# A two-layer decoder on one Trainium2 core: the last output projection by seven block products in place of eight, and the last scan begun sooner

## The chip, the core and the metric

The kernel runs on one core of a Trainium2 chip. Five engines of the core work side by side, each through its own queue of instructions in order: PE (TensorE, matrix products), DVE (VectorE), ACT (ScalarE), POOL (GpSimd) and SP (SyncE, which here only issues DMAs). They meet at semaphores. Data comes from HBM by DMA into SBUF (128 partitions); matrix products land in PSUM. The metric is the device time of one execution in microseconds (us); the lower the better.

## The reference: what is computed

There are 512 tokens of width 2048 and two residual layers: differential attention, then RWKV-7 time mixing. The change lies at the end of the second.

```python
def rwkv7_mixer(h, ...):
    p = h @ w_in                                  # 2048 -> 4*2048 + 192
    p = p + (token_shift(p) - p) * mu
    r, k, v, g, dw, da = jnp.split(p, RW_SPLITS, axis=-1)
    ...
    y = wkv7_scan(rh, heads(decay), kh, vh, -kk, kk * ah)     # 32 heads of 64, over 512 tokens
    ...                                           # normalised per head, weighted, bonus term added
    y = y.reshape(B, T, RW_WIDTH).astype(h.dtype) * jax.nn.silu(g)
    return y @ w_out, v_first                     # 512 x 2048 times 2048 x 2048

x = x + out                                       # the residual
```

## The kernel before

**Products of split numbers.** Every large product takes float32 data in three passes. Each operand is cast to a shorter float format (`hi`, ACT), and the rest is taken off by a subtraction (`lo = x - hi`, DVE). `mm3` (line 106) then issues hi·hi, hi·lo and lo·hi into one PSUM tile. `split_w` (line 87) does the cast (L96) and the subtraction (L97) for a piece of weights that `load_w` (line 73) has brought by a DMA from the SP queue. The raw weights have three buffers (`wraw`), `wh` and `wl` two each. `split_row` (line 403) does the same for a row of activations, into tiles `hH` and `hL` with sixteen buffers each.

**The order of the work.** The program is written in the framework's tile language. Each instruction gets a priority by its place in the program, raised by a fixed number inside `high_priority`; a scheduler fixes the order of every engine's queue when the program is built, by priority among those instructions whose inputs it holds ready and whose buffers it holds free. `issue_after(m)` puts instructions of the same engine behind matmul m.

**The second layer** walks over 16 pairs of heads (128 channels each). For each pair the projections `proj(0..3, j)` (48 matmuls each) give r, k, v and the gate; a small triangular solve runs on DVE (`t_solve`, line 830, tile `Tm`), its result goes through HBM (`td`) and comes back in 4 DMAs as `TT`; `t_combine` (line 860) finishes it with two groups of 32 small matmuls (tile `px`); `scan_pair` (line 950) then steps through 8 chunks of 64 tokens, with three small matmuls a chunk (L961, L972, L979, tile `sm`). In a chunk the state `VS` is updated on DVE (L983) from `sm` and from `Sg`, which POOL makes by one scaling (L970) after two copies into `SA` (L967). So that PE is not held up, these steps are strewn among the large products by a `Chain` (line 114): `tick` counts the matmuls of `mm3`, and every `yield n` in a chain's steps asks for n matmuls before the next step. A chain only counts once the chain before it is done. For the last pair (j = 15) the call is `chain(g, j, p, 80, 4, 4)`: 80 matmuls before the first step, 4 between the steps of a chunk.

**The last output projection.** `y` (channels x tokens) is 16 K tiles of 128 channels. Rows 0 to 13 lie in HBM (`yd2`); they are loaded and split once. Row 14 is made just before, row 15 only when the last scan is done. The weights are taken in four blocks of 512 columns; each block has four PSUM tiles (4 x 128 tokens; two of them are called `pp`, two `pt`) and runs over K in 8 pieces of 2 K tiles: one cast and one subtraction of 128 x 1024, then 24 matmuls of 128 x 512. At the end of a block four additions on DVE (L1126) add the residual, which comes by DMA from `xd`, and the results are stored from the ACT queue. In the first block the last scan runs between the matmuls; its row 15 joins as the last K tile.

Of the kernel before, what the change touches and what calls it, by code (L numbers as in the profile page):

```python
# [13 lines left out]
F32 = mybir.dt.float32  # L14
F32R = mybir.dt.float32r
# [3 lines left out]
ALU = mybir.AluOpType  # L19
# [4 lines left out]
P = 128  # L24
D = 2048
T = 512
KT = D // P
NT = T // P
# [10 lines left out]
AHEAD, SCAN, SOLVE = 2000, 3000, 4000  # L39
# [63 lines left out]
    return [(win, h * 256, 256), (win, D + h * 256, 256)]  # L103


def mm3(nc, out, aH, aL, bH, bL, start, stop, g=None):
    for a, b, s, e in ((aH, bH, start, False), (aH, bL, False, False), (aL, bH, False, stop)):
        m = nc.tensor.matmul(out, a, b, start=s, stop=e)  # L108
        if g:
            tick(g, m)  # L110
    return m
# [909 lines left out]
def group_norm(g, j, p):  # L1021
    p.chain.finish(g)
    nc, w, yc = g.nc, g.work, p.yc
    NG = 2 * NT
    sq = w.tile([P, NG, C], F32, name="ysq", tag="thg", bufs=1)
    nc.scalar.activation(sq[:], yc[:], AF.Square)
    var = g.small.tile([P, NG], F32, name="var", tag="var")
    nc.vector.reduce_sum(var[:], sq[:], AX.X)
    nc.vector.tensor_scalar(var[:], var[:], 1.0 / C, GN_EPS, ALU.mult, ALU.add)
    rs = g.small.tile([P, NG], F32, name="rsg", tag="rsg")  # L1030
    rsqrt(g, rs[:], var[:], NG, "r8")
    nc.vector.tensor_mul(yc[:], yc[:], rs[:, :, None].to_broadcast([P, NG, C]))
# [8 lines left out]
    nc.vector.scalar_tensor_tensor(p.y[:], ps[:], g.prm["hgw"][:, j : j + 1], p.y[:], ALU.mult, ALU.add)  # L1041


def layer1(g, aps):
    nc, tc = g.nc, g.tc
    with ExitStack() as cx:
# [23 lines left out]
        for j in range(D // P):  # L1070
# [30 lines left out]
                gated(g, j - LAG, pairs[j - LAG], gate(g, j - LAG, proj(3, j - LAG)))  # L1101
            if j + 1 < D // P:
                r = receptances(j + 1)
        chain(g, j, p, 80, 4, 4)
        gated(g, j - 2, pairs[j - 2], gate(g, j - 2, proj(3, j - 2)))
        gps = proj(3, j - 1)
        group_norm(g, j - 1, pairs[j - 1])
        finish_y(g, j - 1, pairs[j - 1])
        row = gated(g, j - 1, pairs[j - 1], gate(g, j - 1, gps), True)
        gt = gate(g, j, proj(3, j))  # L1110
        rows = split_rows(g, g.yd2, ("r", "k", "th0", "th1"), 1, j - 1) + [row]

        def all_rows(n, _):
            if n >= KT and len(rows) < KT:
                group_norm(g, j, p)
                finish_y(g, j, p)
                rows.append(gated(g, j, p, gt, True))

        yH, yL = Rows(rows, 0), Rows(rows, 1)
        for cb in range(4):  # L1120
            cs = slice(cb * 512, (cb + 1) * 512)
            pts = unit_tok(g, yH, yL, [(aps["rw_w_out"][0], cb * 512, 512)], 512, 2, more=all_rows)
            for t in range(NT):
                xr = w.tile([P, 512], F32, name="xr1", tag=("r", "k", "th0", "th1")[t], bufs=1)
                nc.sync.dma_start(out=xr[:], in_=g.xd[t * P : (t + 1) * P, cs])
                nc.vector.tensor_add(xr[:], xr[:], pts[t][:])  # L1126
                nc.scalar.dma_start(out=aps["out"][t * P : (t + 1) * P, cs], in_=xr[:])


@with_exitstack  # L1130
def body(ctx, tc, nc, aps):
    g = Ctx()
    g.nc, g.tc = nc, tc
    g.last, g.first = None, []
    g.chains, g.later, g.state = [], [], None
# [39 lines left out]
```

## Time and profile before

| | |
|---|---|
| Time, median of three runs (lowest to highest) | 2236.04 us (2233.57 to 2239.77) |
| The profiled execution's own time | 2235.41 us |
| Its span, first to last instruction | 2233.7 us |
| mean granted TensorE clock in it | 0.995 |
| DMA over the span | mean 100 GB/s |
| The four blocks of the last projection (us) | 55.06, 43.52, 43.52, 43.56 |
| DVE, ACT, POOL busy in the second block (us) | 12.53, 8.44, 0.00 |

The profile is of one execution. Busy time of an engine counts its instructions from start to end; matmuls are pipelined, so a matmul lasts longer than the distance to the next one, and the distance is the better measure of what it costs. A row of a timeline gives start and duration (us), engine, line, operation, written tile, read tiles and shape, in square brackets the idle time ahead of it and what ended that. A row that ends with x12 holds twelve instructions that follow each other. In a grouped view a row ends with the count, the busy time, the mean duration (ns) of one, and the idle time of that engine ahead of them. A row for a tile gives the minimum, the median and the maximum duration (ns).

### The profile page before, as it was taken

The numbers are of one execution on the slowest core, as the hardware profiler recorded it, in microseconds if no ns is written. First come the engines' busy times: TensorE is split into PE (matmuls) and PEld (weight loads), VectorE is DVE, ScalarE is ACT, GpSimd is POOL, SyncE is SP. The second block draws the span as 40 slices with busy tenths as digits, with TensorE's granted clock in tenths as the row PEclk, the third lists the DMA queues.
The fourth block names the chain that finished last, engine by engine and source line by source line (L and its number), as shares of the span: only waits on it lengthen the run. The fifth ranks groups of instructions, "written<-read, shape, count | busy, mean of one in ns | idle before, by whom it ended". The sixth has DMA issues, their size and how long they took to land. (4 is left out here: it accounts for less than half of the span.)

```text
span 2233.7 us, 33774 instructions
## 1 busy us (share of the span) xinstructions
PE 2184.1 (98%) x12260; PEld 1770.4 (79%) x12260; DVE 1374.9 (62%) x3666; ACT 1005.1 (45%) x2065; POOL 297.4 (13%) x672
## 2 busy tenths in 40 slices
PE   8999999999999999989999999999999999999999
PEld 6888888888888878877777777787777777777887
DVE  5555646455564664245667787777777877777322
ACT  5443434334343452225455555555455556545211
POOL 0000000000000000000323133333322233331000
PEclk9999999999999999999999999999999999999999
DMA  6222222222222254332423333333333333435333
GB/s 180 94 86 96 85 95 95 85 95 85 95 85 95 91 194 132 115 113 74 102 68 83 88 88 86 86 91 99 90 81 81 97 88 78 107 93 156 123 132 113
DMA packets 290730, 224.46 MB, mean 100 GB/s; under 512 B 47732, under 2 KB 255748, under 8 KB 290564
## 3 DMA queue, kind: packets, MB, share of 16 engines
q1 hardware_dynamic: 275892, 195.74, 30.2%
q0 software_dynamic: 6144, 10.84, 2.0%
q10 hardware_dynamic: 8528, 15.73, 2.0%
q8 instruction: 96, 1.57, 0.3%
q14 instruction: 70, 0.57, 0.1%
HBM read 202.26 MB, written 19.99 MB: 99 GB/s over the span
## 5 line engine op out<-in xcount | busy, mean ns | idle before, releaser
L97 DVE TENSOR_TENSOR wl<-wraw,wh 128x1024 fp32r<-128x1024 f32 (+2 forms) x325 | 396.0, 1219 | 498.8 <-ACT wh L96 498.2
L96 ACT CAST wh<-wraw 128x1024 fp32r<-128x1024 f32 (+2 forms) x325 | 340.0, 1046 | 659.1 <-PE pp L108 453.9
L108 PE MATMUL pp<-wh,hH 128*128 128x512 f32 x1408 | 554.7, 394 | 6.0 <-ACT hH L586 5.3
L108 PE MATMUL pp<-wh,hL 128*128 128x512 f32 x1408 | 552.6, 393 | 0.0
L108 PE MATMUL pp<-wl,hH 128*128 128x512 f32 x1408 | 552.0, 392 | 0.0
L108 PE MATMUL pp<-hL,wh 128*128 128x512 f32 (+1 forms) x1056 | 430.3, 407 | 0.1
L108 PE MATMUL pp<-hH,wl 128*128 128x512 f32 (+1 forms) x1056 | 428.3, 406 | 0.4 <-DVE wl L97 0.4
L108 PE MATMUL pp<-hH,wh 128*128 128x512 f32 (+1 forms) x1056 | 425.1, 403 | 2.1 <-DVE mixt L629 1.8
L108 PEld LDWEIGHTS pp<-wh,hH 128*128 128x128 f32 x1408 | 265.1, 188 | 60.2 <-ACT hH L586 6.0
L108 PEld LDWEIGHTS pp<-wh,hL 128*128 128x128 f32 x1408 | 265.0, 188 | 54.2 <-DVE hL L587 0.6
L108 PEld LDWEIGHTS pp<-wl,hH 128*128 128x128 f32 x1408 | 265.2, 188 | 52.3
L108 PEld LDWEIGHTS pp<-hH,wh 128*128 128x128 f32 (+1 forms) x1056 | 199.4, 189 | 40.6 <-DVE mixt L629 2.2
L108 PEld LDWEIGHTS pp<-hL,wh 128*128 128x128 f32 (+1 forms) x1056 | 199.4, 189 | 37.5 <-DVE hL L587 1.7
L108 PEld LDWEIGHTS pp<-hH,wl 128*128 128x128 f32 (+1 forms) x1056 | 199.6, 189 | 34.0 <-DVE wl L97 0.8
L850 DVE SCALAR_TENSOR_TENSOR tmpl<-LT,Tm 128x60 f32<-128x60 f32 (+24 forms) x496 | 133.1, 268 | 10.7
L967 POOL COPY SA<-VS 64x64 f32<-64x64 f32 x224 | 58.0, 259 | 445.6 <-DVE VS L983 388.1
L678 POOL MEMSET rmask<- 128x512 bf16 x1 | 0.5, 525 | 832.9 <-DVE nb L339 832.9
L852 DVE TENSOR_TENSOR Tm<-Tm,tmpl 128x60 f32<-128x60 f32 (+24 forms) x496 | 104.6, 211 | 10.9
L983 DVE SCALAR_TENSOR_TENSOR VS<-sm,gam,Sg 64x64 f32<-64x64 f32 x192 | 54.3, 283 | 51.9 <-PE sm L979 47.6
L964 ACT COPY rhs<-sm 64x64 f32<-64x64 f32 x256 | 52.6, 205 | 66.7 <-PE sm L961 64.4
L974 ACT COPY VS<-sm 64x64 f32<-64x64 f32 x256 | 52.6, 206 | 59.0 <-PE sm L972 55.2
L970 POOL TENSOR_SCALAR Sg<-SA,gam 128x64 f32<-128x64 f32 x96 | 72.1, 751 | 9.3
(269 smaller groups left out, 2801.3 us busy)
## 6 DMA issues: line engine op xcount, KB each, us to landing
wraw<-in_rw_w_in_dram SPq DMA_DIRECT2D x128, 512.0 KB, 4.0
wraw<-in_da_w_in_dram SPq DMA_DIRECT2D x254, 256.0 KB, 3.0
wraw<-in_da_w_out_dram SPq DMA_DIRECT2D x32, 512.0 KB, 3.6
wraw<-in_rw_w_out_dram SPq DMA_DIRECT2D x32, 512.0 KB, 3.6
LT<-ltd POOLq DMA_DIRECT2D x64, 132.0 KB, 2.9
yr<-yd SPq DMA_DIRECT2D x28, 256.0 KB, 3.8
xq<-in_x_dram SPq DMA_DIRECT2D x16, 256.0 KB, 5.2
xd<-xq ACTq DMA_DIRECT2D x16, 256.0 KB, 2.9
```

What stands on the lines that cost most here:

```text
L96: nc.scalar.copy(hi[:, ks], raw[:, ks])
L97: nc.vector.tensor_sub(lo[:, ks], raw[:, ks], hi[:, ks].bitcast(F32))
L108: m = nc.tensor.matmul(out, a, b, start=s, stop=e)
L678: nc.gpsimd.memset(g.rmask[:], 1.0)
L850: nc.vector.scalar_tensor_tensor(tt, LT[:, i : i + 1, i + 1 :].to_broadcast([P, s, n]), n2[:, i : i + 1], Tm[:, 0:s, i : i + 1].to_broadca ...
L852: nc.vector.tensor_add(Tm[:, 0:s, i + 1 :], Tm[:, 0:s, i + 1 :], tt)
L964: nc.scalar.copy(rhs[r_, :], sm[r_, h * C : h * C + C])
L967: nc.gpsimd.tensor_copy(p.SA[r_, c - 1, :], VS[r_, c, h, :])
L970: nc.gpsimd.tensor_scalar(Sg[:], p.SA[:, c - 1, :], p.gam[:, c : c + 1], None, ALU.mult)
L974: nc.scalar.copy(VS[r_, c, h, :], sm[r_, P : P + C])
L983: g.state = nc.vector.scalar_tensor_tensor(VS[r_, c + 1, h, :], s_, p.gam[r_, c : c + 1], Sg[r_, :], ALU.mult, ALU.add)
```

## The change

The projection runs in two halves of 1024 columns (`half_out`). In each, the 512 tokens, K tiles 0 to 13 and 1024 columns are cut in halves (256 tokens, 7 K tiles, 512 columns), and the four quadrants of the result are made from seven products of sums of blocks (Winograd's form of Strassen's scheme). K tiles 14 and 15 are multiplied plainly.

The sums of the `y` blocks (S1 to S4) are made once on POOL (`load_forms`), from blocks loaded from HBM into the buffers of `hH` and `hL`; they are kept in float32 and split anew ahead of each product (`split_form`). The sums of the weight blocks are made on POOL too (`comb`), for each half: Ts = W12 - W11, then W22 - Ts, then Ts - W11 (W11 loaded a second time), then W21 - Ts. The 7 K tiles of a block are taken in groups of 1, 2, 2 and 2 (`KS`). A product of one group is a cast and a subtraction of the form, a cast and a subtraction of the weights, and 12 matmuls (6 in the group of one). `take` adds a PSUM pair to the result tile, which already holds the residual. The last scan's delay is 24 matmuls in place of 80, its gaps 5, 5 and 6 in place of 4, and its norm and row 15 are made in two steps at fixed places of the first half (`next(last, None)`).

```diff
+KS = ((0, 1), (1, 2), (3, 2), (5, 2))
+def load_forms(g, src):
...
+    for i, (k0, n) in enumerate(KS):
+        for at, nm in enumerate(("11", "21", "22", "S1", "S2", "S4", "12")):
+            f[nm] = g.hp.tile([P, n, 256], F32, name="f" + nm, tag=("hH", "hL")[(at + i) % 2])
+            if nm in PLACES:
...
+                nc.sync.dma_start(out=f[nm][:], in_=src[r0 : r0 + n * P, t * 256 : t * 256 + 256].rearrange(
+                    "(k p) t -> p k t", p=P))
+        add = lambda o, a, b, op: nc.gpsimd.tensor_tensor(out=f[o][:], in0=f[a][:], in1=f[b][:], op=op)
+        add("S1", "21", "22", ALU.add)
+        f["S3"] = f["21"]
+        add("S3", "11", "21", ALU.subtract)
+        add("S2", "S1", "11", ALU.subtract)
+        add("S4", "12", "S2", ALU.subtract)
...
+@urgent
+def split_form(g, f):
...
+    g.turn = 1 - g.turn
+    hi = w.tile(list(f.shape), F32R, name="fH", tag=("xH", "f")[g.turn], bufs=1)
+    lo = w.tile(list(f.shape), F32R, name="fL", tag=("xL", "l")[g.turn], bufs=1)
+    nc.scalar.copy(hi[:], f[:])
+    nc.vector.tensor_sub(lo[:], f[:], hi[:].bitcast(F32))
...
+def half_out(g, w, dst, forms, rows, cb, last):
...
+    def prod(out, i, form, wt, first, end):
+        aH, aL = split_form(g, forms[i][form])
+        wh, wl = split(wt, KS[i][1])
+        n = KS[i][1]
+        for k in range(n):
+            for t in range(2):
+                s = slice(t * P, (t + 1) * P)
+                mm3(nc, out[t][:], aH[:, k, s], aL[:, k, s], wh[:, k, :], wl[:, k, :], first and k == 0,
+                    end and k == n - 1, g, True)
...
+    def take(nm, ps):
+        for t in range(2):
+            nc.vector.tensor_add(acc[nm][:, t, :], acc[nm][:, t, :], ps[t][:])
...
+    def comb(o, a, b):
+        with g.tc.high_priority(offset=AHEAD):
+            nc.gpsimd.tensor_tensor(out=o, in0=a, in1=b, op=ALU.subtract)
+
+    N = len(KS)
+    y = Y()
+    for i, (k0, n) in enumerate(KS):
+        b11 = load(k0, n, c1)
+        prod(X, i, "11", b11, i == 0, i == N - 1)
+        b12 = load(k0, n, c2)
+        comb(Ts[i], b12[:], b11[:])
+        prod(y, i, "S1", Ts[i], i == 0, i == N - 1)
+    take("11", X)
+    take("22", y)
+    next(last, None)
+    b22 = []
+    for i in (0, 2):
+        for a in (i, i + 1):
+            b22.append(load(NS + KS[a][0], KS[a][1], c2))
+            comb(Ts[a], b22[a][:], Ts[a])
+            prod(X, a, "S2", Ts[a], False, a == N - 1)
+        if i == 2:
+            take("12", X)
+        for a in (i, i + 1):
+            prod(y, a, "S4", b22[a], False, False)
+        if i == 0:
+            next(last, None)
+    wt = split(load(2 * NS, 2, c2), 2)
+    plain(y, 0, wt, False)
+    take("12", y)
+    store("12")
+    z = Y("pc")
+    plain(z, 2, wt, True)
+    take("22", z)
+    for i, (k0, n) in enumerate(KS):
+        b11 = load(k0, n, c1)
+        comb(b11[:], Ts[i], b11[:])
+        prod(X, i, "S3", b11, False, i == N - 1)
+    take("22", X)
+    store("22")
...
+    def second(i):
+        b21.append(load(NS + KS[i][0], KS[i][1], c1))
+        comb(Ts[i], b21[i][:], Ts[i])
+        prod(y, i, "12", b21[i], i == 0, False)
+    def fourth(i):
+        prod(X, i, "22", Ts[i], False, False)
+    for f, i in ((second, 0), (second, 1), (fourth, 0), (fourth, 1), (second, 2), (fourth, 2)): f(i)
...
-        chain(g, j, p, 80, 4, 4)
+        chain(g, j, p, 24, 5, 6)
...
-        rows = split_rows(g, g.yd2, ("r", "k", "th0", "th1"), 1, j - 1) + [row]
...
+        forms = load_forms(g, g.yd2)
+        rows = [row]
+        def norm_last():
+            group_norm(g, j, p)
+            yield
+            finish_y(g, j, p)
+            rows.append(gated(g, j, p, gt, True))
+            yield
+        last = norm_last()
+        for cb in range(2):
+            half_out(g, aps["rw_w_out"][0], aps["out"], forms, rows, cb, last)
```

More of the change, by code (lines that the diff above doesn't have):

```diff
@@ L103, in qk_cols, with mm3 @@
     return [(win, h * 256, 256), (win, D + h * 256, 256)]
-def mm3(nc, out, aH, aL, bH, bL, start, stop, g=None):
+def mm3(nc, out, aH, aL, bH, bL, start, stop, g=None, skip=False):
     for a, b, s, e in ((aH, bH, start, False), (aH, bL, False, False), (aL, bH, False, stop)):
-        m = nc.tensor.matmul(out, a, b, start=s, stop=e)
+        m = nc.tensor.matmul(out, a, b, start=s, stop=e, skip_group_check=skip)
         if g:
@@ L1041, in finish_y @@
     nc.vector.scalar_tensor_tensor(p.y[:], ps[:], g.prm["hgw"][:, j : j + 1], p.y[:], ALU.mult, ALU.add)
+NS = 7
+KS = ((0, 1), (1, 2), (3, 2), (5, 2))
+PLACES = {"11": (0, 0), "12": (0, 1), "21": (1, 0), "22": (1, 1)}
+def load_forms(g, src):
+    nc = g.nc
+    forms = []
+    for i, (k0, n) in enumerate(KS):
+        f = {}
+        for at, nm in enumerate(("11", "21", "22", "S1", "S2", "S4", "12")):
+            f[nm] = g.hp.tile([P, n, 256], F32, name="f" + nm, tag=("hH", "hL")[(at + i) % 2])
+            if nm in PLACES:
+                t, k = PLACES[nm]
+                r0 = (k * NS + k0) * P
+                nc.sync.dma_start(out=f[nm][:], in_=src[r0 : r0 + n * P, t * 256 : t * 256 + 256].rearrange(
[6 more added lines that the diff above has]
+        add("S4", "12", "S2", ALU.subtract)
+        forms.append(f)
+    return forms
@@ L1110, in layer1 @@
         gt = gate(g, j, proj(3, j))
-        rows = split_rows(g, g.yd2, ("r", "k", "th0", "th1"), 1, j - 1) + [row]
[L1113 to L1127, printed above, removed]
+        forms = load_forms(g, g.yd2)
[9 more added lines that the diff above has]
+            half_out(g, aps["rw_w_out"][0], aps["out"], forms, rows, cb, last)
 @with_exitstack
@@ L1134, in body @@
     g.last, g.first = None, []
-    g.chains, g.later, g.state = [], [], None
+    g.chains, g.later, g.state, g.turn = [], [], None, 0
     g.const = ctx.enter_context(tc.tile_pool(name="const", bufs=1))
```

47 lines of the change are left out of this document (added).

## The prediction

> **What bounds the kernel now.** I read the page's busy shares first, then busy time by stretch, then the chain of waits over the last projection.
>
> ```profile
> span 2233.7 us, 33774 instructions
> PE 2184.1 (98%) x12260; PEld 1770.4 (79%) x12260; DVE 1374.9 (62%) x3666; ACT 1005.1 (45%) x2065; POOL 297.4 (13%) x672
> ```
>
> ```profile
> core 0: us, PE busy (x) PEld busy (x) DVE busy (x) ACT busy (x) POOL busy (x), PEclk, DMA share, GB/s
> ...
> 2044.11:2099.17 55.06, 54.55 (x301) 41.66 (x302) 29.86 (x60) 22.10 (x55) 7.68 (x20) 1.00 0.40 129
> 2099.17:2142.69 43.52, 43.52 (x194) 36.04 (x193) 12.53 (x13) 8.44 (x8) 0.00 (x0) 1.00 0.43 145
> ```
>
> ```profile
> 2037.53 1.02 PE px L880 x32
> ...
> 2099.17 2.72 PE pp L108 x12
> 2101.89 2.72 PE pt L108 x12
> ```
>
> PE sets the end. From the second column block on, groups of twelve matmuls follow each other without a hole, 0.2267 us (2.72 / 12) a matmul, at full clock; a block is 192 x 0.2267 = 43.52. DVE and ACT are busy 12.53 and 8.44 of that, POOL not at all. The first block takes 11.54 more, nearly all busy: the scan's own matmuls. What the change removes here comes off the end; what it adds elsewhere is free only while it stays under the matmuls.
>
> **The matmuls.** Per half: seven products x 7 K tiles x 2 token tiles x 3 = 294, plain part 2 x 2 x 3 x 4 quadrants = 48, together 342, or 77.5 us against 87.04 for two blocks now. Over both halves 84 fewer than 768: **-19.0 us**.
>
> **The copies.** Their prices:
>
> ```profile
> L96 ACT CAST wh<-wraw 128x1024 fp32r<-128x1024 f32 x8 | 8.4, 1054 | 35.0 <-PE pt L108 30.7 <-DVE xr L1126 4.4
> L97 DVE TENSOR_TENSOR wl<-wraw,wh 128x1024 fp32r<-128x1024 f32 x8 | 9.8, 1225 | 29.9 <-ACT wh L96 29.9
> L407 ACT CAST hH<-yr 128x512 fp32r<-128x512 f32 x28 | 16.3, 620 | 6.9 <-DMA yr<-yd 6.8
> L408 DVE TENSOR_TENSOR hL<-yr,hH 128x512 fp32r<-128x512 f32 x28 | 18.6, 687 | 2.6 <-ACT hH L407 2.6
> L597 ACT CAST sHup<-upw x16: 388/406/408, 1037.3 to 1895.2; 96x256 fp32r<-96x256 f32 x16
> L598 DVE TENSOR_TENSOR sLup<-upw,sHup x16: 406/410/422, 1037.8 to 1897.0; 96x256 fp32r<-96x256 f32 x16
> L1126 DVE TENSOR_TENSOR xr<-xr,pt 128x512 f32<-128x512 f32 x3 | 2.1, 688 | 0.0
> ```
>
> A group of two K tiles needs on DVE 0.69 (form) + 1.23 (weights) = 1.92, a group of one 0.41 + 0.69 = 1.10. Seven products of 1.10 + 3 x 1.92 and two plain pieces of 1.23 are 50.5 us per half, where two blocks now have 19.6. The sixteen additions of `take` are 11.0 more. All of it fits into 77.5; the question is lead time:
>
> ```profile
> 2109.66 0.39 PE L108 MATMUL pt<-wh,hL 128*128 128x512 f32 x1
> ...
> 2110.09 1.05 ACT L96 CAST wh<-wraw 128x1024 fp32r<-128x1024 f32 x1 [4.34 <-PE pt L108]
> ...
> 2111.18 1.23 DVE L97 TENSOR_TENSOR wl<-wraw,wh 128x1024 fp32r<-128x1024 f32 x1 [4.17 <-ACT wh L96]
> ```
>
> The last matmul on a buffer fills its slot until 2109.66 + 0.23 = 2109.89; the next cast starts 0.20 later and the low part is there at 2112.41, 2.52 behind the slot. Now 24 matmuls (5.44 us) of the other buffer cover that. In the change the form's cast (0.62) goes ahead on ACT, its buffer free one matmul earlier, so the low part comes 2.9 behind. It is covered by the group between and the two hi·hi products that can go first (0.45): 2.72 + 0.45 = 3.17, enough, if that group has 12 matmuls; 1.36 + 0.45 = 1.81, 1.1 too little, if it has six. A group of two directly behind a group of one comes six times per half (once in the 11/S1 block, twice in S2/S4, once in S3, twice in 12/22): 6.6 us. DVE has 0.8 free of each 2.72, so most additions go into holes, but the four of the first `take` pair (2.75 together) meet groups of one: 1.8. Sum 8.4 per half, **+16.8 us**. The ends: 0, if the copies are started earlier than I see; 6.6 + 16 x 0.69 = 17.6 per half, if every addition delays a copy in the queue behind it.
>
> **The sums on POOL.** No two-operand operation runs on POOL in this trace. The nearest rows are its affine selections, one operand in, one out:
>
> ```profile
> L816 POOL TENSOR_SCALAR_AFFINE_SELECT G<-G 64x1024 f32<-64x1024 f32 x32 | 37.1, 1158 | 0.1
> ...
> L970 POOL TENSOR_SCALAR Sg<-SA,gam x96: 439/445/1817, 1131.7 to 2070.5; 128x64 f32<-128x64 f32 x96
> ...
> L814 POOL TENSOR_SCALAR_AFFINE_SELECT G<-G x32: 652/657/1047, 1069.1 to 1982.1; 64x512 f32<-64x512 f32 x32
> ```
>
> That is 0.16 + 0.98 per 1000 elements a partition. Bounds for `comb` of 1024: 1.16, if the second operand comes along free; 2.16, if it doubles the slope (1.16 for 512). The following rows make me take the upper: POOL reads through something that it can't even share with DVE, so two operands of its own should pass in turn.
>
> ```profile
> 1150.23 1.26 DVE L97 TENSOR_TENSOR wl<-wraw,wh 128x1024 fp32r<-128x1024 f32 x1
> 1150.51 1.34 POOL L970 TENSOR_SCALAR Sg<-SA,gam 128x64 f32<-128x64 f32 x1
> ```
>
> ```profile
> 1109.83 1.16 POOL L816 TENSOR_SCALAR_AFFINE_SELECT G<-G 64x1024 f32<-64x1024 f32 x1
> 1109.91 1.35 DVE L853 TENSOR_TENSOR Tm<-Tm,LT 128x256 f32<-128x256 f32 x1
> ...
> 1111.18 1.21 DVE L97 TENSOR_TENSOR wl<-wraw,wh 128x1024 fp32r<-128x1024 f32 x1
> ...
> 2022.58 0.42 DVE L853 TENSOR_TENSOR Tm<-Tm,LT 128x256 f32<-128x256 f32 x1
> ```
>
> Above, POOL's scaling (0.445 by its median) takes 1.34 and ends 0.36 behind the copy that was running. Below, a DVE product that takes 0.42 in the last solve lasts 1.35 and ends 0.27 behind POOL's selection. So a DVE operation that reads two SBUF tensors and a POOL operation that reads SBUF go one after the other. Every copy `lo = x - hi` is of that kind, and so is every `comb`. Behind a held copy stand, on DVE, the additions of `take` (and `take`'s reader, the next product into that PSUM pair) and in the first half the scan's update L983; PE waits for all three. Their joint load per half is 50.5 + 4 x (1.16 + 3 x 2.16) = 81.1 us: more than the 77.5 of matmuls.
>
> Block by block: two groups of two with one `comb` need 2 x 1.92 + 2.16 = 5.99 against 5.44 on PE, 0.55 too much, nine times (three blocks): 4.9. Two groups of one: 2.20 + 1.16 - 2.72 = 0.64, three times: 1.9. In the S3 block every group has a `comb`: 1.92 + 2.16 - 2.72 = 1.36 three times and once 0.90: 5.0. Of these 11.8 some 1.8 is made ahead under the plain matmuls (48 x 0.2267 = 10.9 with 2.45 of copies). Left 10.0 per half, **+20 us**. The ends: at 1.16 and 0.66 only the S3 block (1.5) and the groups of one (0.4) are over, 1.9 per half; if each `comb` comes whole into the copy's way beyond DVE's free 0.8 or 0.26, it is 12 x 1.36 + 4 x 0.90 = 19.9 per half.
>
> The Trainium skill gives a price: "GPSIMD Engine Reference" (3. Performance versus the Vector engine) states 4497 ns for a float32 `tensor_tensor` of 2048, an estimate of 2.25 us for 1024; the sum would be 2 us higher by it. "SBUF — State Buffer" (Who interferes with whom) states that a DVE instruction with at most one SBUF input does not contend with GpSimd. The trace agrees with its row here, which has one input and its usual 0.44 (435 ns in the row of `TT` further down) inside a selection of 1.16:
>
> ```profile
> 1117.59 1.16 POOL L816 TENSOR_SCALAR_AFFINE_SELECT G<-G 64x1024 f32<-64x1024 f32 x1
> 1118.06 0.44 DVE L874 STREAM_TRANSPOSE T<-TT 64x256 f32<-64x256 f32 x1
> ```
>
> By that rule the additions of `take` (one operand in PSUM) stay out of the joint load; without it the load would be 11 us per half higher, and the sum 22.
>
> **The forms and the scan.** Fourteen loads of rows with their casts and subtractions go; sixteen loads and sixteen POOL sums come, 4 x (0.66 + 3 x 1.16) = 16.6 us. The loads wait for buffers that the last gate projection frees one by one before 2044, so about half the sums lie ahead of the projection, on an idle port. The other 8 us meet a half in which the scan's 11.5 us of matmuls give the copies time: 0 to +8, I take **+2**. The scan's earlier start:
>
> ```profile
> 2023.07 0.37 SPq L854 DMA_DIRECT2D td<-Tm  x1
> 2027.28 1.81 SPq L866 DMA_DIRECT2D TT<-td  x4
> 2029.18 9.44 SPq L78 DMA_DIRECT2D wraw<-in_rw_w_out_dram  x3
> ...
> L874 DVE STREAM_TRANSPOSE T<-TT x2: 428/435/442, 2029.1 to 2030.2; 64x256 f32<-64x256 f32 x2
> ```
>
> The four `TT` loads already go as soon as `td` has landed, ahead of the next weight loads on SP, so the shorter delay moves no DMA there, and the solve is done with POOL's DMAs by then. The `px` products can't start before 2030.2 + 0.44 = 2030.6: 6.9 earlier than 2037.5, not the 56 x 0.2267 = 12.7 asked for. If PE's queue has them at 2037.5 - 12.7 = 2024.8, it stands up to 5.8 us there with the gate's matmuls behind; if the order knows of the late load, 0. I take 1. The wider gaps can save at most the first block's waits, 0.5 (PE idle) to 3 (within rows that overlap); I take 1. Together **0**.
>
> **Loads and tail.** A half loads 39 K tiles of 256 KB in place of 32, 10.2 MB, with 2.1 each for residual and store: about 148 GB/s over 97 us, as now (145).
>
> ```profile
> wraw<-in_rw_w_out_dram SPq DMA_DIRECT2D x20, 512.0 KB, 3.6
> ```
>
> Three buffers hide the landing of 3.6; without that cover each of the 22 loads would show what is left of it behind its group's 2.72, about 1. The end keeps one addition (0.69) and a store behind the last matmul. Both 0.
>
> Sum: -19.0 + 16.8 + 20 + 2 + 0 = +19.8 on the profiled execution's own 2235.4, **2255 us**; that execution is 0.6 below the median of the runs, so it moves nothing.
>
> **Rivals.** *The copies stay hidden* (faster): PE keeps its stream, POOL's sums run in DVE's free 0.8 and under the plain matmuls, and only a third of the copies' waits (6) is left: 2235.4 - 19 + 6 = 2222. For it: DVE and ACT have room in sum, and S2 and S4 go by pairs of groups, so that sums can run ahead. Against it: two buffers, twelve matmuls, and the joint load of 81.1. It decides from a `comb` that doesn't hold up copies. *POOL's sums cost the lower bound*: -19 + 16.8 + 4 + 2 = +3.8, 2239. For it: on DVE a second operand costs nothing (0.687 for 512). *The scan is held up as well* (slower yet): each of the six `Sg` waits for a `comb` of 2.16 that itself waited for a copy of 1.23, 3.4 late against the two gaps of 2.3 before L983 needs it, with its own 0.45 some 1.5 each, 9 in all, and `px` stands its 5.8 in place of 1: 2255 + 13.8 = 2269 us. For it: `Sg` is held up today (1.82 at most); against: a `comb` rarely lies right ahead of it.
>
> **How the numbers follow.** Forecast 0.55 (by itself 2243 to 2268), copies hidden 0.20, lower bound 0.13, scan held up 0.12. A measurement here can tell about 0.3%, 6.7 us, from no change. Faster 0.20, same 0.13 (2239 lies within), slower 0.67. The range, 2224 to 2276, takes in all but the outer halves of the first and last rival.
>
> **What would show it.** Right: in the second half PE waits at groups of two, most in the S3 block, for DVE's subtractions (`wl`), POOL's `TENSOR_TENSOR` of 1024 at about 2.2 us or stretched by a copy, DVE subtractions of 1024 with durations well over 1.23 us, a half of 95 to 98 us, `px` at 2030 or later. Wrong: a half near 78 to 82 us with PE unbroken; sums of 1.2 us; or PE waiting for weight loads, which I put at nothing.

## The result and the profile after

The changed kernel takes 2272.22 us (median of four runs, 2268.58 to 2273.45), the kernel before beside it 2236.28 (four runs, 2233.57 to 2239.77): a ratio of 1.0157, 95% interval 1.0138 to 1.0176. It is 36 us slower; 2255 was forecast. The profiled execution took 2273.45. The head of its page:

```profile
span 2271.4 us, 33975 instructions
...
PE 2186.5 (96%) x12176; PEld 1759.8 (77%) x12176; DVE 1478.3 (65%) x3752; ACT 1047.6 (46%) x2135; POOL 398.7 (18%) x720
```

PE has the 84 matmuls less (12176 after, 12260 before) and yet as much busy time; DVE has 103 us more, POOL 101.

To place the loss I cut both traces at the same events: the matmul that makes `Y` of pair 14 (the code ahead of it is the same), the first matmul of the projection, the matmul that makes `Y` of pair 15 (the end of the last scan), the end of the first half (of the second block before) and the end of the last matmul. The columns are start and end, length, busy time with instructions of PE, PE's weight loads, DVE, ACT and POOL, then granted clock, DMA share and GB/s. First the kernel before, then the changed one:

```profile
2012.81:2042.47 29.66, 29.66 (x212) 24.60 (x212) 24.41 (x65) 12.49 (x21) 0.00 (x0) 1.00 0.43 123
2042.47:2076.26 33.79, 33.28 (x181) 23.74 (x179) 16.94 (x31) 19.26 (x51) 7.68 (x20) 1.00 0.51 161
2076.26:2142.69 66.43, 66.43 (x348) 55.19 (x348) 26.03 (x42) 12.89 (x14) 0.00 (x0) 1.00 0.38 128
2142.69:2229.57 86.88, 86.88 (x385) 71.73 (x383) 23.67 (x24) 15.82 (x15) 0.00 (x0) 1.00 0.37 122
```

```profile
2016.18:2052.96 36.78, 34.34 (x263) 27.22 (x262) 25.84 (x69) 14.11 (x33) 9.14 (x12) 1.00 0.52 156
2052.96:2092.59 39.63, 28.86 (x105) 21.85 (x104) 26.83 (x26) 16.33 (x37) 37.84 (x31) 0.83 0.41 135
2092.59:2167.97 75.38, 67.91 (x331) 50.98 (x331) 63.36 (x81) 31.38 (x46) 24.10 (x11) 1.00 0.39 131
2167.97:2267.18 99.21, 84.71 (x343) 62.41 (x341) 78.77 (x72) 40.24 (x55) 36.59 (x15) 1.00 0.33 110
```

I call the first three rows together the first part: 129.9 us before, 151.8 after. The second half goes from 86.9 to 99.2. Together that is 34.2; the other 3.4 between the two starts (2012.81, 2016.18) lie in unchanged code. Its start moves by itself: one program, profiled twice (b5 and c1 below), had it at 2022.52 and 2012.57. So all stretches below are counted from that event. PE, which stood 0.5 us in these stretches before, now stands 35.2 (251.0 - 215.8 busy), and in the second row its clock is 0.83.

Who PE waits for, in the first half and in the second (total us, times, longest):

```profile
PE sm L979 <- ACT VS L974: 7.2, 2, 4.7
PE pp L108 <- DVE wl L97: 5.2, 6, 2.0
PE pt L108 <- DVE wl L97: 4.1, 3, 2.0
```

```profile
PE pp L108 <- DVE wl L97: 11.1, 10, 2.2
PE pt L108 <- DVE wl L97: 2.4, 2, 1.8
PE pt L108 <- ACT wh L96: 0.8, 2, 0.5
```

In the second half it is the weights' low parts, 13.5 of 14.3 us; in the first a scan step, L979, takes almost as much (7.2 us beside 9.3), in two waits. The groups of the second half on DVE and POOL show why the low parts are late (count | busy us, mean ns | idle before and what ended it):

```profile
L97 DVE TENSOR_TENSOR wl<-wraw,wh 128x1024 fp32r<-128x1024 f32 x14 | 21.9, 1562 | 2.6 <-ACT wh L96 2.6
L1080 DVE TENSOR_TENSOR fL<-f,fH 128x512 fp32r<-128x512 f32 x12 | 15.5, 1289 | 6.3 <-ACT fH L1079 6.3
...
L1080 DVE TENSOR_TENSOR fL<-fS,fH 128x512 fp32r<-128x512 f32 x9 | 6.1, 684 | 3.6 <-ACT fH L1079 3.6
L1128 DVE TENSOR_TENSOR acc<-acc,pt 128x512 f32<-128x512 f32 x9 | 5.8, 679 | 4.7 <-PE pt L108 4.7
```

```profile
L1138 POOL TENSOR_TENSOR T<-wraw,T 128x1024 f32<-128x1024 f32 x6 | 17.4, 2916 | 15.7 <-DMA wraw<-in_rw_w_out_dram 15.7
...
L1138 POOL TENSOR_TENSOR wraw<-T,wraw 128x1024 f32<-128x1024 f32 x3 | 7.2, 2397 | 5.0 <-DMA wraw<-in_rw_w_out_dram 5.0
```

The subtractions with both operands in SBUF have swollen: 1562 for 1225 ns, 1289 for 690 (the row of b1 below). The nine out of `fS` (684) lie where no POOL sum runs and have not, nor have the additions of `take`, with one operand in PSUM (679). A POOL sum of 1024 takes 2.40 us where nothing holds it, 2.92 on average in the first of these groups. One meeting, from the timeline: the subtraction starts inside the sum, takes 2.39 us and ends 0.55 behind it.

```profile
2169.16 2.67 POOL L1138 TENSOR_TENSOR T<-wraw 128x1024 f32<-128x1024 f32 x1 [5.59 <-DMA wraw<-in_rw_w_out_dram]
2169.99 2.39 DVE L1080 TENSOR_TENSOR fL<-f,fH 128x512 fp32r<-128x512 f32 x1 [0.42 <-ACT fH L1079]
```

POOL itself often waits for a load ahead of a sum (5.59 us here). That this is what makes PE wait in this half is a rival; the chain of work that ended last, taken over the half, speaks against it, for it has DVE's subtractions in it and neither a load nor POOL:

```profile
by line: PE pp L108 33.2%; DVE wl L97 20.0%; PE pt L108 16.9%; issue 11.1%; DVE fL L1080 8.5%; DVE acc L1128 4.7%; ACT fH L1079 3.0%; ACT wh L96 2.4%; ACTq L1134 0.3%; ACTq L96 0.1%; DVEq L97 0.0%
```

### The profile page after: what moved, and what is told of

Its sections match the earlier page's. It is cut to its first block, busy times and chain, and to the rows that moved or that the text cites. A ratio compares the mean times of both kernels' runs of the same rounds, so it can differ in the third digit from the quotient of the medians.

```text
span 2271.4 us, 33975 instructions
## 1 busy us (share of the span) xinstructions
PE 2186.5 (96%) x12176; PEld 1759.8 (77%) x12176; DVE 1478.3 (65%) x3752; ACT 1047.6 (46%) x2135; POOL 398.7 (18%) x720
## 5 line engine op out<-in xcount | busy, mean ns | idle before, releaser
L97 DVE TENSOR_TENSOR wl<-wraw,wh 128x1024 fp32r<-128x1024 f32 (+2 forms) x329 | 411.7, 1251 | 410.2 <-ACT wh L96 409.4
L108 PE MATMUL pp<-wh,hH 128*128 128x512 f32 x1288 | 507.4, 394 | 6.0 <-ACT hH L586 5.3
L108 PE MATMUL pp<-wh,hL 128*128 128x512 f32 x1288 | 505.6, 393 | 0.5 <-DVE hL L587 0.5
L108 PE MATMUL pp<-wl,hH 128*128 128x512 f32 x1288 | 505.2, 392 | 0.0
L108 PEld LDWEIGHTS pp<-wh,hH 128*128 128x128 f32 x1288 | 242.6, 188 | 56.0 <-ACT hH L586 6.2
L108 PEld LDWEIGHTS pp<-wh,hL 128*128 128x128 f32 x1288 | 242.5, 188 | 50.1 <-DVE hL L587 1.2
L108 PEld LDWEIGHTS pp<-wl,hH 128*128 128x128 f32 x1288 | 242.6, 188 | 48.0
L967 POOL COPY SA<-VS 64x64 f32<-64x64 f32 x224 | 61.0, 272 | 398.9 <-DVE VS L983 374.1
L852 DVE TENSOR_TENSOR Tm<-Tm,tmpl 128x60 f32<-128x60 f32 (+24 forms) x496 | 104.7, 211 | 10.9
L983 DVE SCALAR_TENSOR_TENSOR VS<-sm,gam,Sg 64x64 f32<-64x64 f32 x192 | 54.2, 283 | 52.9 <-PE sm L979 48.6
L974 ACT COPY VS<-sm 64x64 f32<-64x64 f32 x256 | 52.8, 206 | 68.1 <-PE sm L972 53.3
```

Source lines behind the costliest of these rows:

```text
L97: nc.vector.tensor_sub(lo[:, ks], raw[:, ks], hi[:, ks].bitcast(F32))
L108: m = nc.tensor.matmul(out, a, b, start=s, stop=e, skip_group_check=skip)
L852: nc.vector.tensor_add(Tm[:, 0:s, i + 1 :], Tm[:, 0:s, i + 1 :], tt)
L967: nc.gpsimd.tensor_copy(p.SA[r_, c - 1, :], VS[r_, c, h, :])
L974: nc.scalar.copy(VS[r_, c, h, :], sm[r_, P : P + C])
L983: g.state = nc.vector.scalar_tensor_tensor(VS[r_, c + 1, h, :], s_, p.gam[r_, c : c + 1], Sg[r_, :], ALU.mult, ALU.add)
```

## The experiments

Twelve runs: ten kernels, then one of them (c1) and the changed kernel (c2) once more. Times are medians beside the kernel before on the same chip. A run without a ratio is a single execution, and so is every stretch (first part, second half); single executions of the kernel before, on all these chips, reach from 2229.95 to 2243.21 us.

| | first part | second half | time | before | ratio (95%) |
|---|---|---|---|---|---|
| before | 129.9 | 86.9 | | 2236.28 | |
| changed | 151.8 | 99.2 | 2272.22 | 2236.28 | 1.0157 (1.0138 to 1.0176) |
| a1 no form sums | 139.1 | 100.6 | 2264.75 | 2236.56 | |
| a2 no weight sums | 136.3 | 85.9 | 2238.24 | 2236.56 | |
| a3 no sums | 130.4 | 85.9 | 2235.52 | 2236.56 | |
| a4 scan sooner alone | 130.0 | 86.9 | 2235.15 | 2236.56 | 1.0002 (0.9987 to 1.0018) |
| b1 POOL writes only | 140.9 | 86.5 | 2251.83 | 2240.36 | |
| b2 no sums, three buffers | 129.3 | 79.6 | 2234.03 | 2240.36 | |
| b3 sums on DVE | 137.0 | 91.6 | 2252.46 | 2240.36 | 1.0064 (1.0042 to 1.0085) |
| b4 the same, three buffers | 139.2 | 87.4 | 2247.48 | 2234.99 | 1.0051 (1.0036 to 1.0065) |
| b5 last scan off POOL | 145.6 | 99.3 | 2273.37 | 2240.36 | |
| c1 b5 again | 149.8 | 101.4 | 2269.60 | 2237.04 | 1.0144 (1.0130 to 1.0158) |
| c2 changed kernel again | 152.2 | 98.9 | 2273.42 | 2237.04 | 1.0160 (1.0146 to 1.0174) |
| c3 a3, forms in row buffers | 129.8 | 84.7 | 2231.59 | 2235.69 | 0.9980 (0.9969 to 0.9991) |

**Which sums cost.** a1 leaves out the sums of the forms (each product takes a plain block of `y`), a2 those of the weights, a3 both; casts, loads of weights and matmuls stay.

```diff
 a1, a3:
-        add("S1", "21", "22", ALU.add)
-        f["S3"] = f["21"]
-        add("S3", "11", "21", ALU.subtract)
-        add("S2", "S1", "11", ALU.subtract)
-        add("S4", "12", "S2", ALU.subtract)
+        f["S1"], f["S3"], f["S2"], f["S4"] = f["22"], f["21"], f["11"], f["12"]
 a2, a3:
-        comb(Ts[i], b12[:], b11[:])
-        prod(y, i, "S1", Ts[i], i == 0, i == N - 1)
+        prod(y, i, "S1", b12, i == 0, i == N - 1)
...
```

> The changed kernel without the sixteen sums of y blocks on POOL: S1, S2, S3 and S4 stand for the loaded blocks 22, 11, 21 and 12, so the output is not the reference's. The loads, all copies, the weight sums and the matmuls stay. Theory (the form sums lie in POOL's queue ahead of the scan's two copies into SA, and PE stands for the scan; the first half lost 10 us more than predicted there, part of it at a granted clock below 1): the time falls from 2272 to 2257 to 2263 us, PE's waits for L974 (7.2 us in the first half) shrink below 3, and the second half stays at 98 to 100 us. Rival (the weight sums hold the scan, and the form sums are hidden but for 2 us, as the prediction took them): 2268 to 2272, with the waits for L974 still there.

> The changed kernel without the weight sums (comb) on POOL: each product multiplies by the loaded block itself, so the output is not the reference's. The loads, the form sums, all copies and the matmuls stay. Theory (copies and weight sums go one after the other, and their joint load sets the pace of a half): the second half falls from 99.4 to 85 to 88 us, the subtractions of 128x1024 come back to 1.23 us, the time falls to 2240 to 2250. Rival (the copies' lead time alone makes the half slow, the sums fit beside them): the second half stays above 95 and the time above 2262.

> The changed kernel without any sum on POOL, form or weight; the products multiply the loaded blocks, so the output is not the reference's. What is left against the kernel before: 84 matmuls fewer, and the copies in groups of twelve and six. Theory (the prediction's term of the copies, 8.4 us a half): second half 84 to 88 us, time 2230 to 2236, hardly below the kernel before, although all sums are gone. Rival (the copies are covered once nothing holds them): second half 77.5 to 79 us and a time of 2214 to 2221.

Without sums the changed kernel is where the kernel before was: 2235.52 beside 2236.56. So the sums take the loss, to within that spread. a1 (28.2 us above its kernel before) and a2 (1.7 above) miss their forecast times by 2 us each, a1 above and a2 below; their waits and second halves came as the theories had them, but for 0.6 us in a1 (100.6 where at most 100 was expected). In the second half only the weight sums count: 85.9 without them, 99.2 with them, 13.3 us. In the first part the form sums alone add 5.9 (a2 - a3), the weight sums alone 8.7 (a1 - a3), both together 21.4 (changed - a3): 6.8 more than their sum. PE's waits for L974 go with that: none in a1, 1.7 us in a2, 7.2 with both. These are differences of single executions; one program's first part differs by 4.2 below (b5, c1). The second half of a3:

```profile
2143.60:2229.50 85.90, 82.56 (x343) 62.94 (x341) 57.89 (x72) 40.03 (x55) 0.00 (x0) 1.00 0.38 132
```

It is 8.4 above the 77.5 of the forecast's matmuls, the very term of the copies, though not all of it is the copies, as b2 and c3 show.

**The scan's start alone**, in the kernel before:

```diff
-        chain(g, j, p, 80, 4, 4)
+        chain(g, j, p, 24, 5, 6)
```

> The kernel before with only the last scan's delay and gaps changed (24, 5, 6 in place of 80, 4, 4). Theory (the px products are bound by the load of TT, and the order of PE's queue knows of it; the prediction took the scan's move at nothing): ratio 0.998 to 1.001, px at 2029 to 2032 with less than 2 us of waiting. Rival 1 (PE stands at px until TT has come): +4 to +6 us, ratio 1.002 to 1.003. Rival 2 (the scan's waits in the first block vanish): -3 us or more.

No difference: 1.0002; `px` runs from 2027.9 to 2030.4, behind a wait of 0.7. `px` and the first scan steps now stand ahead of the projection, and what is added there falls out of the first block.

**What POOL does to DVE.** b1 replaces each `comb` by POOL instructions of about the same length that write the same tile and read nothing (the weight sums are left out of what is computed).

```diff
-            nc.gpsimd.tensor_tensor(out=o, in0=a, in1=b, op=ALU.subtract)
+            for end in (None, None, 256):
+                nc.gpsimd.memset(o[:, :, :end], 0.5)
```

> The changed kernel with each weight sum replaced by POOL memsets of its tile that read nothing and take about as long (2.5 memsets of 0.956 us for 128x1024, 2.4 us as the unhindered sum took); the products multiply constants, so the output is not the reference's. Form sums, loads, copies and matmuls stay, and a product still waits until POOL has written its tile. Theory (it is the reading of SBUF that POOL and the copies can't do at once): the subtractions of 128x1024 come back to 1.23 us, the second half falls from 99.2 to 86 to 90 us, the time to 2238 to 2250. Rival (POOL's own time in front of the casts makes the wait, whatever it reads): second half 96 to 100, time above 2262. The Trainium skill, in SBUF — State Buffer (Who interferes with whom), states that a GpSimd instruction that only writes does not contend with a DVE instruction of two SBUF inputs; by that rule the first comes out.

The second half, its subtractions on DVE and its POOL instructions:

```profile
L97 DVE TENSOR_TENSOR wl<-wraw,wh 128x1024 fp32r<-128x1024 f32 x14 | 17.1, 1224 | 5.6 <-ACT wh L96 5.5
...
L1080 DVE TENSOR_TENSOR fL<-f,fH 128x512 fp32r<-128x512 f32 x12 | 8.3, 690 | 8.1 <-ACT fH L1079 8.1
```

```profile
L1139 POOL MEMSET T<- 128x1024 f32 x12 | 11.4, 954 | 17.4 <-DVE wl L97 17.1
...
L1139 POOL MEMSET T<- 128x256 f32 x2 | 0.6, 312 | 0.1
```

POOL is about as long on a tile (2 x 0.954 + 0.312 = 2.2 us), at the same place in its queue, and DVE is back at 1224 ns; the half is 86.5, not 99.2. The first part is 140.9, 4.6 above a2's, hardly more than one program varies there; the time of the single execution, 11.5 above its kernel before, lies just over the range expected. These instructions need no loaded operand either, but a load that POOL waits for would not shorten a DVE instruction: it is POOL's reading of SBUF that holds the copies. The Trainium skill, "SBUF — State Buffer" (Who interferes with whom), says as much: a DVE instruction with two SBUF inputs contends with a GpSimd instruction that reads SBUF, not with one that only writes it. The trace agrees on both counts: 1562 against 1224 ns.

b3 puts all sums on DVE, where they can't collide with a copy but take their own time; the whole projection is computed.

```diff
-        add = lambda o, a, b, op: nc.gpsimd.tensor_tensor(out=f[o][:], in0=f[a][:], in1=f[b][:], op=op)
+        add = lambda o, a, b, op: nc.vector.tensor_tensor(out=f[o][:], in0=f[a][:], in1=f[b][:], op=op)
...
-            nc.gpsimd.tensor_tensor(out=o, in0=a, in1=b, op=ALU.subtract)
+            nc.vector.tensor_tensor(out=o, in0=a, in1=b, op=ALU.subtract)
```

> The changed kernel, whole, with all sums (forms and weights) on DVE in place of POOL. Theory (a sum costs its own length on the shared way; a DVE sum of 128x1024 takes 1.23 us where POOL's took 2.37 unhindered): DVE has 50.5 + 11.0 + 4 x (0.69 + 3 x 1.23) = 79 us a half, with the lead time of 8.4 about 90 to 94 us, first part 132 to 140, time 2243 to 2254: 20 to 28 us faster than the changed kernel, still no faster than the kernel before. Rival (one engine must do in a row what two took in turns, so nothing is won): second half 98 or more, time 2266 or more.

From 1.0157 to 1.0064, and a second half of 91.6: the engine that is already the fuller one does the sums better, 1.22 us for a `comb` of 1024 in place of 2.40 that shut the copies out.

**The lead time.** b2 is a3 with a third pair of buffers for the split forms, and in the second half for the split weights.

```diff
-    g.turn = 1 - g.turn
-    hi = w.tile(list(f.shape), F32R, name="fH", tag=("xH", "f")[g.turn], bufs=1)
-    lo = w.tile(list(f.shape), F32R, name="fL", tag=("xL", "l")[g.turn], bufs=1)
+    g.turn = (g.turn + 1) % 3
+    hi = w.tile(list(f.shape), F32R, name="fH", tag=("xH", "f", "th0")[g.turn], bufs=1)
+    lo = w.tile(list(f.shape), F32R, name="fL", tag=("xL", "l", "th1")[g.turn], bufs=1)
...
+        hi, lo = third[:, 0, :n], third[:, 1, :n]
```

> The run without any sum (a3_no_sums: 2235.5 us, second half 85.9) with a third buffer for split weights in the second half and a third for split forms; the output is not the reference's either. Theory (the 8.4 us a half are lead time: two buffers and groups of six and twelve matmuls): second half 78 to 80.5 us, time about 2228 to 2231, PE waiting for wl less than a third as often. Rival (DVE's queue sets it, with the additions of take among the copies): second half 83 to 86, time 2232 to 2236.

```profile
2148.43:2228.00 79.57, 79.57 (x343) 64.03 (x341) 56.00 (x70) 39.34 (x53) 0.00 (x0) 1.00 0.41 138
```

PE is busy for all of the 79.57 us; the time of the one execution came out 3 us over the range expected. So lead time was 85.9 - 79.6 = 6.3 of a3's 8.4, and a buffer removes it. What is left above 77.5 is 2.0, with no wait at all.

b4 gives the same third pair to b3.

> All sums on DVE as in b3_sums_on_dve, and on top a third pair of buffers: for the split forms everywhere, for the split weights in the second half. The whole projection is computed. Two theories of what b3 still loses in its second half (91.55 us against 77.5 of matmuls). (1) Lead time: with two buffers each low part comes too late behind a short group, whatever the engines' load. Without any sums the third buffer took the second half from 85.9 to 79.6, 6.3 us; here it then takes off as much, 91.55 - 6.3 = 85.3 us (84 to 87). (2) Load of DVE: copies and sums on one engine, 50.5 + 4 x (0.69 + 3 x 1.23) = 68.0, and with eight additions of 0.69 and eight more behind them 79 us, are over the 77.5 of the matmuls; buffers can't lower this, and the half is 89 to 92 us. First part (Y of pair 14 to the end of the first half): b3 had 136.95; only the forms have a third pair there, so 135 to 137 by either. Whole time against the kernel before: b3's ratio was 1.0064; by (1) 6 to 8 us less, 1.003 to 1.004; by (2) 1.005 to 1.007. If the third buffer lets DVE run ahead under the plain matmuls as well, the half falls to 79 to 82 and the ratio to about 1.001.

The half is 87.4: 4.2 of the 6.3 came, between the two theories. The four S3 products run there without a wait (2201.53 to 2211.32). The stretch round them shows what is left:

```profile
2196.00:2220.00 24.00, 21.24 (x91) 16.52 (x90) 21.80 (x28) 10.64 (x15) 0.00 (x0) 1.00 0.43 144
```

DVE is busy for 21.80 of 24.00 there, and in the block behind S3 PE waits 1.4 us for the cast and 1.3 for the low part in a third buffer. That DVE's load binds where every group has a sum fits this, but isn't shown: two sums for that block also start 1.0 and 0.7 us late because of a load, and no run parts the two. The first part became 2.3 longer, which neither theory has; its clock in the scan's stretch is 0.90 where b3's is 1.00 (33.1 us against 31.7); why isn't settled. The whole kernel stays at 1.0051, not told apart from b3.

**The last scan.** In the first half PE's longest wait is for ACT's copy of the scan's state. Timeline of the changed kernel:

```profile
2072.04 1.61 POOL L1063 TENSOR_TENSOR fS<-f,fS 128x512 f32<-128x512 f32 x1
...
2072.57 2.16 DVE L97 TENSOR_TENSOR wl<-T,wh 128x1024 fp32r<-128x1024 f32 x1
2073.61 3.31 POOL L1138 TENSOR_TENSOR T<-wraw 128x1024 f32<-128x1024 f32 x1
2076.87 0.52 POOL L967 COPY SA<-VS 64x64 f32<-64x64 f32 x2
...
2077.13 0.50 ACT L974 COPY VS<-sm 64x64 f32<-64x64 f32 x2 [4.59 <-POOL SA L967]
...
2077.68 0.79 PE L979 MATMUL sm<-VS,BKT 128*128 128x128 f32 x2 [4.66 <-ACT VS L974]
```

POOL's copies into `SA` (L967) stand in its queue behind a form sum and a `comb` that a DVE subtraction holds (3.31 us). ACT may not write `VS` before they have read it; ACT waits 4.59, PE 4.66. b5 moves the copies and `Sg` of the last scan to ACT; the whole projection is computed.

```diff
-                nc.gpsimd.tensor_copy(p.SA[r_, c - 1, :], VS[r_, c, h, :])
+                (nc.scalar.copy if j == D // P - 1 else nc.gpsimd.tensor_copy)(p.SA[r_, c - 1, :], VS[r_, c, h, :])
...
+            if j == D // P - 1:
+                nc.scalar.activation(Sg[:], p.SA[:, c - 1, :], AF.Copy, scale=p.gam[:, c : c + 1])
...
```

> The changed kernel, whole, with the last scan's two copies into SA and its scaling Sg on ACT in place of POOL; nothing is left out. Theory (the form and weight sums stand in POOL's queue ahead of the scan's copies; ACT's copy into VS waits for these, and PE for that): the stretch from the end of the scan before to the end of the first half falls from 151.8 by 7 to 13 us, PE's waits for L974 vanish, the granted clock of the first half goes from 0.94 to 0.98 or more, time 2259 to 2265. Rival (the sums slow the copies there as in the second half, and the scan's waits only share that time): less than 4 us, time 2268 or more. The second half stays at 99 in both.

These waits were gone and the first part was 6.2 shorter, less than the 7 to 13 expected, and the whole time no lower (33.0 us above its own kernel before, where the changed kernel has 35.9). So the same program ran again in five rounds, beside the changed kernel:

> The same program as b5_scan_off_pool (the whole projection; the last scan's SA copies and its Sg on ACT in place of POOL), now timed in five rounds beside the changed kernel in the same stay on the chip. In b5's one look the first part (Y of pair 14 to the end of the first half) was 145.6 us against 151.8, yet the whole time was no lower. (1) The scan held up behind POOL's sums costs what the first part showed: this comes 4 to 7 us below the changed kernel, ratio to the kernel before 1.0126 to 1.0139 where the changed kernel has 1.0157. (2) The wait is only handed on, to the low parts of weights that are late anyway: this lies within 2 us of the changed kernel, 1.0148 to 1.0166, and b5's shorter first part was a drift of one execution.

> The changed kernel as it is, as the yardstick for c1_scan_off_pool_again on the same chip. By every theory 1.0138 to 1.0176 of the kernel before, 2268 to 2276 us; its first part near 151.8 us and its second half near 99.2 us, in one more profiled execution. If the first part comes within 2 us of 151.8 here, the 145.6 of b5 was no drift.

The second and third stretch (projection's first matmul to the scan's end, and on to the end of the half), c1 and then c2:

```profile
2047.93:2078.83 30.90, 25.32 (x106) 17.72 (x104) 27.72 (x25) 19.04 (x49) 28.03 (x14) 0.94 0.56 190
2078.83:2162.37 83.54, 71.91 (x332) 54.18 (x332) 67.35 (x82) 32.00 (x46) 29.52 (x14) 0.94 0.36 119
```

```profile
2054.28:2093.99 39.71, 28.89 (x105) 21.86 (x104) 25.46 (x26) 16.30 (x37) 37.91 (x31) 0.83 0.42 137
2093.99:2169.69 75.70, 67.89 (x331) 50.98 (x331) 63.92 (x81) 31.39 (x46) 24.10 (x11) 1.00 0.39 130
```

The scan's stretch is 8.8 us shorter, and 7.8 of it are given back in the next one: sums that had been done in the scan's shadow are now done later (POOL 29.52 for 24.10), and PE runs there at a clock of 0.94; in b5, the same program, it was 1.00 and that stretch 78.80. In whole time 3.8 us remain between the medians. The ratios' intervals overlap (1.0144 against 1.0160), but the runs themselves hardly do: the four of c1 end at 2271.49 us, the five of c2 begin at 2271.48. So the hold-up is shown; its price is near 4 us, at an estimate from these nine runs 1.5 to 6.4.

**The matmuls' own pace.** In b2 nothing waits, and yet the half has 2.0 us too much. In a3 the products of split forms follow each other at about 0.2335 us, those of split rows at 0.2267 to 0.23. c3 is a3 with the split forms in two fixed pairs of row buffers (like a3 it leaves out every sum).

```diff
+    g.fh = [g.hp.tile([P, 512], F32R, name="fH", tag="hH") for _ in range(2)]
+    g.fl = [g.hp.tile([P, 512], F32R, name="fL", tag="hL") for _ in range(2)]
...
-    hi = w.tile(list(f.shape), F32R, name="fH", tag=("xH", "f")[g.turn], bufs=1)
-    lo = w.tile(list(f.shape), F32R, name="fL", tag=("xL", "l")[g.turn], bufs=1)
+    hi = g.fh[g.turn][:, : n * 256].rearrange("p (k t) -> p k t", k=n)
+    lo = g.fl[g.turn][:, : n * 256].rearrange("p (k t) -> p k t", k=n)
```

> a3_no_sums with one edit: the split forms (hi and lo) are written into two fixed pairs of row buffers, the same kind of tile that the split rows of y lie in, in place of four tiles of the work pool. Like a3 it leaves out every sum of forms and of weights, so its output is not the reference's product. The traces of the changed kernel, of a3 and of b2 show the products of split forms at 0.2335 us from one matmul to the next, also where nothing waits and DVE is idle, and the products of split rows beside them at 0.2267 to 0.23, as in the kernel before: 294 x 0.0068 = 2.0 us a half that the forecast does not have. (1) It is the place of the stationary tile: the spacing falls to 0.227 to 0.230 here, a3's second half of 85.9 us becomes 84.0, its whole time 3 to 4 us less. (2) It comes with the form of the product (two token tiles that take turns at every K tile, shorter groups): spacing 0.233 to 0.234, second half 85 to 87 us, whole time as a3's 2235.5 within 2 us of the kernel before.

From the chains of work that ended last, the same 24 products of forms in a3 and in c3 (start, length, what):

```profile
2175.06 5.61 PE pp L108 x24
```

```profile
2169.68 5.47 PE pp L108 x24
```

0.2338 a matmul in a3, 0.2279 in c3, with the same instructions. The half fell by 1.2, to 84.7, less than the 2.0 expected. The whole is 4.1 us below its kernel before; a3, at 1.0 below, is a single execution, so the 3 us between them aren't told apart from its spread. It is the buffer that the split forms lie in; what about it (the address, or that it is fixed) was not tried. The weights' buffer counts as well: 24 products of split rows take 5.59 us in b2 (2187.43 to 2193.02), with the weights in its third buffer, and 5.45 in a3 (2186.11 to 2191.56).

No version that computes the whole beats the kernel before. a3, c3 and b2 show the room if the sums were free, and it is small: 1.0, 4.1 and 6.3 us, of which only c3's is clear of noise.

## Why the prediction was right, and where it was short

The sign and the mechanism (POOL's sums and DVE's copies in turn) were right, the forecast 17 us too low. The second half lost 12.3 where 8.9 was forecast, the first part 21.9 where 10.9 was: most of what was missed lies there. Its terms beside the runs, changes from the kernel before in us:

| term | forecast | measured | from |
|---|---|---|---|
| matmuls | -19.0 | -19.0, and +4.0 for the slower pace | 2 x 294 x 0.0068; b2, c3 |
| lead time of the copies, first half | +8.4 | +8.0 | remainder: a3 - before = 0.5, less -9.5 and 2.0 |
| lead time of the copies, second half | +8.4 | +6.3 | a3 - b2 |
| weight sums, second half | +10 | +13.3 | changed - a3 |
| weight sums, first half | +10 | +8.7 | a1 - a3 |
| form sums | +2 | +5.9 | a2 - a3 |
| both kinds of sums together | 0 | +6.8 | remainder; with the scan off POOL near 4 come back (c1) |
| scan's start | 0 | 0 (1.0002) | a4 |
| sum | +19.8 | +34.0 | the stretches above: 34.2 |

The first part's rows are made from remainders, so that their sum had to come out; the +8.0 also holds the 0.7 at `px` and a clock of 0.93 in a3's scan stretch (25.8 us).

**The copies.** "1.1 too little" at six places, 6.6, was the lead time (6.3, and a buffer removes it). The 1.8 for the first pair of `take` did not show; the slower pace filled its place, so that a3's 85.9 agrees with the forecast's 77.5 + 8.4 partly by luck.

**The weight sums.** The mechanism was right: POOL's reads and the two-operand copies go one after the other. The price was too low: 2.16 for a sum of 1024 came from a selection with one operand and a doubled slope; the trace has 2.40, and 1.27 for 512. With these the same count gives 9 x 0.80 + 3 x 0.75 + 3 x 1.60 + 1.01 = 15.3, less 1.8 made ahead, 13.5: the second half's 13.3. The Trainium skill's "GPSIMD Engine Reference" (3. Performance versus the Vector engine), at an estimate of 2.25, was nearer, though still short. That most of the waiting would lie in the S3 block was wrong: the four blocks of the second half have 4.7, 3.5, 3.2 (S3) and 2.8 us of waits. So that the count's sum comes out at 13.5 is partly luck.

**The step that failed** is "about half the sums lie ahead of the projection, on an idle port. The other 8 us meet a half in which the scan's 11.5 us of matmuls give the copies time". POOL was busy for only 9.1 us ahead of the projection, 3.1 of it with form sums (the four of the group of one), and for 37.8 of the 39.6 of the scan's stretch. The forms' sums alone cost 5.9 there, and with the weight sums they fill POOL's queue so that the scan's own POOL instructions come late. I had that as the rival "the scan is held up as well" (2269, 3 us from the result), but by `Sg`, which L983 needs; in the trace it goes by the `SA` copies, which ACT's L974 must wait for, a hazard of a write behind a read, in two long waits and not six short ones. And `px` waited 0.7, not 5.8. So that rival's sum is near by luck.

**The scan's start** was right: `px` starts 16.8 us behind `Y` of pair 14 (24.7 before), held by the late `TT` as forecast, and PE waits 0.7 us there, near the 1 that was taken:

```profile
L880 PE MATMUL px<-T,G x32: 191/191/212, 2033.0 to 2035.2; 32*32 32x32 f32 x32
```

The loads, put at nothing, cost PE nothing without sums: b2's half has them all and PE never stands.

## What to carry to other kernels

Work moved to an idle engine is not free when it reads what a busier neighbour reads: price it as serial with the neighbour's two-operand instructions, and compare with doing it on the neighbour itself. A queue that is nearly empty has tenants too: list the short instructions in it (here two copies a scan step) and who waits for them, also for the right to overwrite. And a scheme that trades matmuls for elementwise work needs buffers by its shortest group: here six places of 1.1 us, removed by a third pair.

## What the runs showed of the hardware

After a wait PE can run at half pace for some microseconds. Behind the 4.66 us wait above (windows of 5 us, then PE's timeline):

```profile
2070.00:2075.00 5.00, 3.02 (x16) 2.15 (x14) 3.86 (x3) 1.99 (x4) 4.92 (x3) 1.00 0.00 0
2075.00:2080.00 5.00, 2.32 (x7) 1.93 (x8) 0.57 (x2) 0.58 (x3) 4.76 (x6) 0.77 0.36 119
```

```profile
2078.70 0.63 PE L108 MATMUL pp<-wh,fH 128*128 128x512 f32 x1
2079.13 0.63 PE L108 MATMUL pp<-wl,fH 128*128 128x512 f32 x1
...
2081.43 0.40 PE L108 MATMUL pt<-wh,fH 128*128 128x512 f32 x1
2081.66 0.40 PE L108 MATMUL pt<-wl,fH 128*128 128x512 f32 x1
```

0.43 us from one matmul to the next, then 0.23 again. The Trainium skill, "TensorE: Matmul & The Clock Gate" (The HAM clock gate), has two rates, full and half, and some 3.4 us of busy time to come back from half; the trace agrees, with 3.4 us from 2077.68 to 2081.1. So a wait costs more than its length: the stretch of the last scan has a mean clock of 0.83 (1.00 before), an estimate of 5 to 7 us lost there (0.17 of the 28.9 busy, or of all 39.6). How long a wait must be isn't settled: behind one of 2.01 us, which ended at 2063.09, the clock was 0.75 from 2065 to 2070, while the second half, with waits of 2.2 at most, has 1.00 (0.98 in c1, with the same longest wait). Which wait sets it off differs between executions: of one program, b5 had 1.00 in the stretch behind the scan and c1 0.94.

A matmul's pace depends on the buffer of its stationary operand (0.2338 against 0.2279 us above), and on that of the moving one (5.59 against 5.45 us for 24, 0.2329 against 0.2271), in products that wait for nothing. And POOL's instructions that only write leave DVE's subtractions alone (1224 ns beside `MEMSET`, 1562 beside sums).
